# A hybrid attention and state-space layer: block 1's tokens loaded later, the output projection's weights split in phase one, four buffers for h, filler from the first slot

## The chip, the cores and the metric

The kernel runs on one core of a Trainium2 chip. The metric is the device time of one execution in microseconds (us), lower is better. Engines are named as in the profile: PE (TensorE matmul), PEld (its weight loads), DVE (VectorE), ACT (ScalarE), POOL (GpSimd), SP (SyncE, which issues nearly all DMAs, in one queue and in order).

## The reference

One layer over 2048 prompt tokens and one step of 32 sample tokens, D = 1024, eight attention heads and eight state-space (SSD) heads of 64, feed-forward width 2816:

```python
def mixer(h, k_past, v_past, ssm_h0, conv_prev, p):
    proj = h @ p['w_in']                     # q, k, v, z, xbc, dt
    ...
    attn = stick_breaking(q, q_pos, k_all, v_all, k_pos).reshape(b, l, D_ATT)
    xbc_c, conv_new = causal_dwconv(xbc, conv_prev, p['ssm_conv_w'], p['ssm_conv_b'])
    xbc_c = jax.nn.silu(xbc_c)
    ...
    y, h_fin = ssd_scan(xh, dt, a, bm, cm, ssm_h0.astype(jnp.float32))
    ...
    y = rmsnorm(y * jax.nn.silu(z), p['g_ssm_out'])
    out = jnp.concatenate([rmsnorm(attn, p['g_attn_out']), y], axis=-1) @ p['w_out']
    return out, k, v, h_fin.astype(ssm_h0.dtype), conv_new

def conv_ffn(h, conv_prev, p):
    gu = h @ p['w_up']
    gate, up = gu[..., :D_FF], gu[..., D_FF:]
    gate_c, conv_new = causal_dwconv(gate, conv_prev, p['ffn_conv_w'], p['ffn_conv_b'])
    act = jax.nn.gelu(gate_c, approximate=True) * up
    return act @ p['w_down'], conv_new

def layer(x, ...):
    m, ... = mixer(rmsnorm(x, p['g_mix_pre']), ...)
    x = x + rmsnorm(m, p['g_mix_post'])
    f, ... = conv_ffn(rmsnorm(x, p['g_ffn_pre']), ...)
    x = x + rmsnorm(f, p['g_ffn_post'])
```

Stick-breaking attention weights a key by sigmoid(z) times the product of 1 - sigmoid over the later keys, which the kernel computes with a scan along the keys.

## The kernel before

All matrices are kept transposed, features on the 128 partitions and tokens along the free axis, in blocks of 512, 512, 512 and 544 tokens (`SBS`, blocks 0 to 3; the last holds the 32 sample tokens too). A product of two float32 matrices is three matmuls: each operand is split into a high part and a low part (hi x hi, hi x lo, lo x hi), in `dense` (L173).

**Weights.** `weight` (called for one chunk of 128 output features) does one of two things. The first time, `raw` loads the float32 chunk (`wraw`, L130), and `divide` makes the high part by a cast on ACT (L153) and the low part by a subtract on POOL (L154), and SP writes both to DRAM (`wS_...`, L157) under a key. Later, `recall` (L145) loads the split pair from there. A tile of the pair is 1024 columns wide in phase one and 512 in the second phase (`unit`); a pair that was written 1024 wide can be recalled in halves under the key with "part".

**Phase one** (`phase_in`) runs per block s: six chunks of the input projection for the convolution branch (weights wbx; ACT evacuates at L403, the DVE multiplies by the row scale r at L409), the convolution on the DVE (L412, L416), silu on ACT and DVE (L388, L389), the V projection (matmuls L441, whose weight is split into wvhi by ACT, L295, and wvlo by the DVE, L296; evacuated by ACT at L448 or L450, and split for the value store by POOL at L462 and L463), the SSD scan (L487 to L596, y matmuls L569), the k and q projections, and the gate z. `prep` (L306 to L323) loads the next block's x and squares it for the norm.

**Attention and what fills it.** `heads(s)` goes through slots (head, key block, group of 128 keys): scores on the PE (z, L899), sigmoid on ACT (L747, L748), the scan prow (L750) on the DVE, a product beta (L755) on POOL or DVE, a transpose on the PE (L918) whose result ACT and DVE split (L922, L923), and the value product (L940), added up by the DVE (L955). The slot i - 2 is finished while slot i is scored (`LOOK` = 2). In between, `fill` takes units from a generator, the filler: in heads(0) the last block's gate and the sample tokens' attention, and in heads(1) to heads(3) the `Tail` of block s - 1: the output projection (`out_units`, weights "out"), its norm and the residual, the split of the normed h (L1088), the up projection with its convolution and gelu, the down projection, with the `finish` of block s - 2 spread among the up projection's units. The last block's tail runs alone at the end. A running sum `debt` gives out the units at `rate` = units / slots.

`finish` handles 256 columns at a time: for each of eight feature chunks it loads h (`xr`, L1415, SP), scales f (L1416, DVE), adds h (L1420, POOL for even chunks and DVE for odd ones) and stores the result (L1421). In heads(2) and heads(3), where it works on blocks 0 and 1, the tile for h has two buffers; the finishes after that take another pool (`late`).

**What sets the order.** The kernel is written as tiles with pools; a scheduler works out each engine's order of instructions from dependencies, the written order and its own estimates, so an edit in one place moves instructions in others. `behind` adds an order between two instructions of one queue.

Of the kernel before, what the change touches and what calls it, by code (L numbers as in the profile page):

```python
# [8 lines left out]
F32 = mybir.dt.float32  # L9
# [8 lines left out]
LOOK = 2  # L18
# [13 lines left out]
P = 128  # L32
D = 1024
KC = D // P
# [35 lines left out]
class Kernel:  # L70
# [56 lines left out]
    def raw(self, src, m):  # L127

        raw = self.wp.tile([P, self.unit, P], F32, name="wraw", bufs=self.rbufs)
        self.nc.sync.dma_start(raw[:, :m, :], src)  # L130
        return raw

    def held(self, pool, tag):
# [131 lines left out]
def phase_in(kn, ctx):  # L265
    nc, tc, a, o = kn.nc, kn.tc, kn.a, kn.o
    pool = lambda name, bufs, **kw: ctx.enter_context(tc.tile_pool(name=name, bufs=bufs, reuse_waits="tile", **kw))
# [6 lines left out]
    wp = kn.wp  # L274
# [31 lines left out]
    def prep(s):  # L306

        t0, nt = SBS[s]
        x = ep.tile([P, KC, 544], F32, name="x")
        for k in range(0, KC, 2):  # L310
            nc.sync.dma_start(x[:, k : k + 2, :nt], a["xT"][:, k : k + 2, t0 : t0 + nt])
        sq = tmp.tile([P, 544], F32, name="sq", bufs=1)
        for k in range(KC):
            if k == 0:
                nc.scalar.activation(sq[:, :nt], x[:, k, :nt], AF.Square)
            else:
                t = tmp.tile([P, 550], F32, name="t")
                nc.scalar.activation(t[:, :nt], x[:, k, :nt], AF.Square)
                nc.gpsimd.tensor_tensor(sq[:, :nt], sq[:, :nt], t[:, :nt], op=ALU.add)
        r = kn.rstd_narrow(rp, psm, "st", [sq], nt, D)  # L320
        for k in range(KC):
            nc.vector.scalar_tensor_tensor(
                x[:, k, :nt], x[:, k, :nt], kn.col(C_GMIX + k), r[:, :nt], op0=ALU.mult, op1=ALU.mult  # L323
            )
        return x
# [41 lines left out]
    for s, (t0, nt) in enumerate(SBS):  # L367
# [7 lines left out]
        raw = ep.tile([P, 6, 550], F32, name="raw")  # L375
# [16 lines left out]
        w = wfirst if s == 0 else None  # L392
        for c, then in zip(order, (*order[1:], None)):
            if w is None:
                w = kn.weight(wp, a["wbx"][c], key=("bx", c))
# [26 lines left out]
            w = ahead  # L422
# [11 lines left out]
            nc.vector.memset(u[:, 32:40], 0.0)  # L434
        for b in range(nb):
            q = min(P, nt - b * P)
            vp = [psd.tile([P, 512], F32, name="o") for _ in range(2)]
            for h in range(2):
                for k in range(KC):
                    for i, (l, rr) in enumerate(((xhi, wv[0]), (xlo, wv[0]), (xhi, wv[1]))):  # L440
                        nc.tensor.matmul(  # L441
                            vp[h][:q, :260], l[k][:, b * P : b * P + q], rr[:, k, h * 260 : h * 260 + 260],
                            start=i == 0 and k == 0, stop=i == 2 and k == KC - 1,
                        )
            v = sd.tile([P, 520], F32, name="v")
            for dst, src in ((v[:q, 0:260], vp[0][:q, :260]), (v[:q, 260:520], vp[1][:q, :260])):
                if s == 0:
                    copy = nc.scalar.activation(dst, src, AF.Copy, scale=rcol[:q, b : b + 1])  # L448
                else:
                    copy = nc.scalar.copy(dst, src)  # L450
            if b == 0:
                silu(owed, copy)
            nc.vector.tensor_tensor(
                u[:q, b * 8 : b * 8 + 8], v[:q, 512:520], kn.cv[:q, C_DTB : C_DTB + 8], op=ALU.add
            )
            tok = t0 + b * P
            nc.sync.dma_start(o["v"][tok : tok + q, :], v[:q, :512])
            if b == 4:
                nc.sync.dma_start(kn.vF[:], v[:DEC, :512])
                continue  # L460
            vs = sd.tile([P, 2, 512], F32R, name="vs", bufs=1)
            nc.gpsimd.tensor_copy(vs[:, 0, :], v[:, :512])  # L462
            nc.gpsimd.tensor_tensor(vs[:, 1, :], v[:, :512], vs[:, 0, :].bitcast(F32), op=ALU.subtract)  # L463
            for e in range(2):
                nc.sync.dma_start(
                    kn.vS[s][:, :, b, e * DH : e * DH + DH].rearrange("h p d -> p h d"),
                    vs[:, e, :].bitcast(F32).rearrange("p (h d) -> p h d", d=DH),
                )
# [228 lines left out]
class Attention:  # L697
# [172 lines left out]
    def heads(self, s, steps, every=None):  # L870

        kn, nc, kp = self.kn, self.kn.nc, self.kp
        nt = SBS[s][1]
        slots = [(h, kc, b) for h in range(NH) for kc in range(s, -1, -1) for b in range(4)]
        att, live, late = [], {}, []
        sq = None
        debt, rate = 0.0, steps / len(slots)
        cur = {}

        def scores(i):  # L880
# [80 lines left out]
        for i in range(len(slots) + LOOK):  # L961
            if i < len(slots):
                scores(i)
            if i >= LOOK:
                debt += rate
                self.fill(int(debt))
                debt -= int(debt)
                values()
                turn(i - LOOK)
                if every is not None:  # L970
                    every(i - LOOK)
# [5 lines left out]
class Tail:  # L977
# [24 lines left out]
    def out_units(self, s, cat, half):  # L1002

        kn, nc, att = self.kn, self.kn.nc, self.att
        c0, c1 = half
        if c0 == 0:
            self.Q = [[self.mp.tile([P, 4, 272], F32, name=f"n{2 * i + e}") for e in range(2)] for i in range(2)]
            self.msq = att.tmp.tile([P, 544], F32, name="sq")
            self.w = {}
        back = list(range(KC - WBUFS * UNIT // KC, KC))  # L1010
        for i, c in enumerate(range(KC) if c0 == 0 else back + list(range(back[0]))):
            m = self.m(c, half)
            w = self.w.pop(c, None)
            if w is None:
                pool = self.keep if self.keep is not None and c not in back else kn.wp
                w = kn.weight(pool, kn.a["wout"][c], key=("out", c), tag=f"w{c}" if pool is self.keep else None)
                if c0 == 0 and (c in back or pool is self.keep):
                    self.w[c] = w
            ps = self.po[0].tile([P, 512], F32, name=self.po[1])
            for k in (4, 5, 6, 7, 0, 1, 2, 3):  # L1020
                kn.dense(ps, w[k : k + 1], cat, c0, c1, k0=k, first=k == 4, last=k == 3, pin=self.pin)
                if k != 3:
                    yield
            nc.scalar.copy(m, ps[:, : c1 - c0])
            if i < KC - 1:
                att.square(self.msq[:, c0:c1], m, i == 0)
            else:
                t = att.tmp.tile([P, 272], F32, name="sqt", bufs=2)[:, : c1 - c0]
                nc.scalar.activation(t, m, AF.Square)
                self.msqs = [self.msq[:, c0:c1], t]  # L1030
            yield
# [364 lines left out]
    def finish(self, s, c0, c1, f):  # L1396
# [10 lines left out]
            yield  # L1407
        for c in range(KC):
            if not self.late:
                h = att.tmp.tile([P, 272], F32, name="xr", bufs=2)[:, :n]  # L1410
            else:
                if c % 2 == 0:
                    pair = self.late.tile([P, 548], F32, name="xr", bufs=4)
                h = pair[:, n * (c % 2) : n * (c % 2) + n]
# [239 lines left out]
```

## Time and profile before

| | before |
|---|---|
| time, median of 3 runs | 2888.32 us (2884.95 to 2894.43) |
| profiled execution, its own time | 2909.14 us |
| its span | 2907.1 us |
| its mean granted clock of the PE | 0.983 |
| phase one, about | 0 to 600 us |
| heads(0), heads(1), heads(2), heads(3), about | 600 to 710, 710 to 1240, 1240 to 1840, 1840 to 2400 us |
| last tail, about | 2400 to 2907 us |

The profile is of one execution. "Idle before, releaser" names what ended an engine's wait; windows give each engine's busy time in a stretch, with the mean clock that the PE was granted (1.00 is full speed). Two stretches of heads(1) and heads(2) do the same work on the output projection: in heads(1) its weights are split, in heads(2) recalled.

### The profile page before, as it was taken

The numbers are of one execution on the slowest core, as the hardware profiler recorded it, in microseconds if no ns is written. First come the engines' busy times: TensorE is split into PE (matmuls) and PEld (weight loads), VectorE is DVE, ScalarE is ACT, GpSimd is POOL, SyncE is SP. The second block draws the span as 40 slices with busy tenths as digits, with TensorE's granted clock in tenths as the row PEclk, the third lists the DMA queues.
The fourth block names the chain that finished last, engine by engine and source line by source line (L and its number), as shares of the span: only waits on it lengthen the run. The fifth ranks groups of instructions, "written<-read, shape, count | busy, mean of one in ns | idle before, by whom it ended". The sixth has DMA issues, their size and how long they took to land.

```text
span 2907.1 us, 46192 instructions
## 1 busy us (share of the span) xinstructions
PE 2803.7 (96%) x16771; PEld 2421.8 (83%) x16771; DVE 1644.0 (57%) x2628; ACT 1223.9 (42%) x2576; POOL 1136.7 (39%) x1073
## 2 busy tenths in 40 slices
PE   7999999988989999999999999989999999999997
PEld 6887879876878888897788888978888879899997
DVE  7685656447664554557455555775666653623333
ACT  5343434246555544455333334654444433321111
POOL 4633231226666666555222223453223224411113
PEclk9999999999999999999999999999999999999998
DMA  8878686878768877786655556666555555755556
GB/s 307 267 270 259 225 246 195 240 233 266 250 222 270 271 270 257 248 282 197 211 176 176 180 182 230 205 202 195 175 170 170 165 188 176 245 177 178 169 178 196
DMA packets 336612, 633.65 MB, mean 218 GB/s; under 512 B 73498, under 2 KB 192930, under 8 KB 327682
## 3 DMA queue, kind: packets, MB, share of 16 engines
q1 hardware_dynamic: 336386, 630.70, 66.5%
q8 instruction: 134, 2.20, 0.3%
q14 instruction: 92, 0.75, 0.1%
HBM read 474.01 MB, written 156.57 MB: 217 GB/s over the span
## 4 chain that ended last, share of the span: by engine, by line
PE 80%; DMA 7%; DVE 7%; ACT 3%; issue 2%; SPq 1%; POOL 1%; DVEq 0%; ACTq 0%; POOLq 0%
PE o L173 40%; PE u L173 12%; PE t L173 11%; PE z L899 4%; PE pa L940 4%; PE pt L918 3%; PE o L441 3%; DMA acB<-acD 1%; DVE prow L750 1%; DMA o_kT<-kf 1%; DMA eA<-acD 1%; DVE xlo L1088 1%; DMA xr<-hS 1%; DVE f L1416 1%; PE u L215 1%
## 5 line engine op out<-in xcount | busy, mean ns | idle before, releaser
L173 PE MATMUL o<-xhi,w 128*128 128x512 f32 (+2 forms) x3968 | 1047.2, 345 | 21.0 <-ACT xhi L346 7.9
L173 PEld LDWEIGHTS o<-xhi,w 128*128 128x128 f32 x3968 | 698.2, 192 | 113.8 <-ACT xhi L346 7.9
L173 PE MATMUL o<-xlo,w 128*128 128x512 f32 (+2 forms) x1984 | 682.1, 344 | 3.7 <-DVE xlo L332 2.5
L755 POOL TENSOR_TENSOR beta<-beta,prow 128x512 f32<-128x512 f32 (+3 forms) x256 | 252.0, 985 | 463.8 <-DVE prow L750 378.4
L173 PEld LDWEIGHTS o<-xlo,w 128*128 128x128 f32 x1984 | 379.7, 191 | 47.0 <-DVE xlo L332 2.9
L173 PE MATMUL u<-xhi,w 128*128 128x512 f32 x1056 | 351.3, 399 | 0.0
L173 PE MATMUL o<-ah,w 128*128 128x512 f32 x992 | 344.7, 403 | 6.2 <-DVE f L1384 6.1
L1336 POOL TENSOR_TENSOR y<-y,gb 128x512 f32<-128x512 f32 (+1 forms) x88 | 116.2, 1320 | 507.9 <-ACT gb L1335 507.8
L154 POOL TENSOR_TENSOR w<-wraw,w 128x512 fp32r<-128x512 f32 (+3 forms) x186 | 244.4, 1318 | 136.1 <-ACT w L153 116.4
L750 DVE TENSOR_TENSOR_SCAN prow<-gam,prow,z 128x513 f32<-128x513 f32 x192 | 245.3, 1278 | 79.1 <-ACT beta L748 76.3
L923 DVE TENSOR_TENSOR wt<-pt,wt 128x512 fp32r<-128x512 f32 (+2 forms) x320 | 192.0, 601 | 160.3 <-ACT wt L922 158.3
L922 ACT CAST wt<-pt 128x512 fp32r<-128x512 f32 (+2 forms) x320 | 167.8, 526 | 220.6 <-PE pt L918 219.6
L173 PEld LDWEIGHTS u<-xhi,w 128*128 128x128 f32 x1056 | 199.6, 189 | 46.9
L173 PEld LDWEIGHTS o<-ah,w 128*128 128x128 f32 x992 | 187.8, 189 | 48.9 <-DVE f L1384 8.1
L747 ACT ACTIVATE gam<-z 128x512 f32<-128x512 f32 (+2 forms) x320 | 172.4, 539 | 102.0 <-PE z L899 63.6
L173 PE MATMUL u<-xlo,w 128*128 128x512 f32 x528 | 209.9, 398 | 0.0
L173 PE MATMUL o<-al,w 128*128 128x512 f32 x496 | 197.3, 398 | 0.0
L173 PE MATMUL t<-xhi,w 128*128 128x272 f32 x960 | 189.5, 293 | 2.0 <-DMA w<-wS_up 1.4
L940 PE MATMUL pa<-wt,v 128*64 128x256 f32 (+3 forms) x1152 | 171.4, 279 | 15.3 <-DVE wt L923 6.0
L1328 DVE SCALAR_TENSOR_TENSOR y<-gb,cv,y 128x512 f32<-128x512 f32 (+1 forms) x176 | 143.5, 815 | 73.6 <-ACT y L1326 70.9
L918 PE MATMUL pt<-ident,beta 128*128 128x128 f32 x1088 | 180.6, 276 | 1.6 <-POOL beta L755 1.0
L153 ACT CAST w<-wraw 128x512 fp32r<-128x512 f32 (+3 forms) x186 | 114.4, 615 | 154.0 <-PE o L173 92.7
(288 smaller groups left out, 4895.1 us busy)
## 6 DMA issues: line engine op xcount, KB each, us to landing
w<-wS_up SPq DMA_DIRECT2D x264, 512.0 KB, 3.5
w<-wS_dn SPq DMA_DIRECT2D x144, 384.0 KB, 3.5
wS_up<-w SPq DMA_DIRECT2D x88, 512.0 KB, 3.3
w<-wS_out SPq DMA_DIRECT2D x78, 512.0 KB, 5.5
wraw<-wup SPq DMA_DIRECT2D x88, 256.0 KB, 4.0
k<-kS SPq DMA_DIRECT2D x80, 256.0 KB, 3.8
v<-vS SPq DMA_DIRECT2D x80, 256.0 KB, 3.9
w<-wS_bx SPq DMA_DIRECT2D x18, 1024.0 KB, 4.9
```

The costliest lines, as they stand in the source:

```text
L154: nc.gpsimd.tensor_tensor(lo, raw[:, :m, :], hi.bitcast(F32), op=ALU.subtract)
L173: mm = nc.tensor.matmul(ps[:, : c1 - c0], l, r, start=first and i == 0 and k == 0, stop=last and i == 2 and k == len(w) - 1, **({"skip_gro ...
L747: nc.scalar.activation(g[:, c0:512], z, AF.Sigmoid, scale=-0.125)
L750: nc.vector.tensor_tensor_scan(back(pr), back(g), z[:, 0:1].to_broadcast([P, n + 1]), self.kn.ones[:, 0:1] if prev is None else prev, op0= ...
L755: eng.tensor_tensor(b[:, :n], b[:, :n], pr[:, c0 + 1 : 513], op=ALU.mult)
L899: mm = nc.tensor.matmul(z[:, :n], q[:, P * b : P * b + P], k[:, :n], start=e == 0, stop=e == 1 and kc < s)
L918: mm = nc.tensor.transpose(t[:, P * j : P * j + P], w[:, P * j : P * j + P], kn.ident[:])
L922: nc.scalar.copy(hi, t)
L923: nc.vector.tensor_tensor(lo, t, hi.bitcast(F32), op=ALU.subtract)
L940: nc.tensor.matmul(av[:m, 2 * P * p + c0 : 2 * P * p + 2 * P], v[:, j, :m], wt[:, rest, j, c0:], start=kc == s and p + j + rest == 0, stop ...
L1328: nc.vector.scalar_tensor_tensor(y[:, :W], gb[:, i : i + W], kn.col(wc + i), y[:, :W], op0=ALU.mult, op1=ALU.add)
L1336: nc.gpsimd.tensor_tensor(y[:, :W], y[:, :W], t, op=ALU.mult)
```

## The change

Four edits. (1) `raw` remembers its load, and the four loads of block 1's x are put behind the load that was the last at that point, the sixth chunk of wbx. (2) In phase one, blocks 1 to 3, ahead of the V projection, eight chunks of wout are loaded, split 1024 wide and written under a new key, and the output projection recalls them in halves. The sixteen splits of 512 columns under the old key are gone. SP's recalls of these weights go from 78 to 94, each of 512 KB, and the writes from sixteen of 512 KB to eight of 1 MB. (3) `xr` has four buffers instead of two in the finishes of blocks 0 and 1. (4) The filler is called in every slot, the first two included, and the rate is worked out for the slots and these two.

```diff
     def raw(self, src, m):
 
         raw = self.wp.tile([P, self.unit, P], F32, name="wraw", bufs=self.rbufs)
-        self.nc.sync.dma_start(raw[:, :m, :], src)
+        self.load = self.nc.sync.dma_start(raw[:, :m, :], src)
         return raw
...
         for k in range(0, KC, 2):
-            nc.sync.dma_start(x[:, k : k + 2, :nt], a["xT"][:, k : k + 2, t0 : t0 + nt])
+            load = nc.sync.dma_start(x[:, k : k + 2, :nt], a["xT"][:, k : k + 2, t0 : t0 + nt])
+            if s == 1:
+                kn.behind(load, kn.load)
...
         for b in range(nb):
             q = min(P, nt - b * P)
+            if 0 < s and b < 3 and 3 * s - 3 + b < KC:
+                kn.weight(wp, a["wout"][3 * s - 3 + b], key=("outw", 3 * s - 3 + b))
...
-        debt, rate = 0.0, steps / len(slots)
+        debt, rate = 0.0, steps / (len(slots) + LOOK)
...
             if i < len(slots):
                 scores(i)
+            debt += rate
+            self.fill(int(debt))
+            debt -= int(debt)
             if i >= LOOK:
-                debt += rate
-                self.fill(int(debt))
-                debt -= int(debt)
                 values()
...
-                w = kn.weight(pool, kn.a["wout"][c], key=("out", c), tag=f"w{c}" if pool is self.keep else None)
+                w = kn.weight(pool, kn.a["wout"][c], key=("outw", c, "part"), tag=f"w{c}" if pool is self.keep else None)
...
             if not self.late:
-                h = att.tmp.tile([P, 272], F32, name="xr", bufs=2)[:, :n]
+                h = att.tmp.tile([P, 272], F32, name="xr", bufs=4)[:, :n]
```

The lines of the kernel after the change stand a few lower: L412, L416 and L389 are L414, L418 and L391 there, and from L441 on four lower (L755 is L759, L848 is L852, L860 is L864, L1420 is L1424).

The first place is the DVE in the first block, from the third L296 on (wvlo, the low part of the V weight; raw is a chunk of the input projection, xc and bc the convolution's outputs). Before, the fourth L296:

```order
L416 SCALAR_TENSOR_TENSOR xc<-raw,cv,xc 128x512 x2
L296 TENSOR_TENSOR wvlo<-wvraw,wvhi 128x1040
L409 TENSOR_TENSOR raw<-raw,r_231 128x512
L389 TENSOR_TENSOR xc<-xc,t 128x512
L537 TENSOR_TENSOR cbm<-y,triu 128x256
L412 TENSOR_SCALAR xc<-raw,cv 128x512
L427 COPY hist<-raw 128x18
L416 SCALAR_TENSOR_TENSOR xc<-raw,cv,xc 128x512 x3
L453 TENSOR_TENSOR u<-v,cv 128x8
```

and in the changed kernel, with the rows around the same L296:

```order
L411 TENSOR_TENSOR raw<-raw,r_231 128x512
L418 SCALAR_TENSOR_TENSOR xc<-raw,cv,xc 128x512
L414 TENSOR_SCALAR xc<-raw,cv 128x512
L429 COPY hist<-raw 128x18
L391 TENSOR_TENSOR xc<-xc,t 128x512
L541 TENSOR_TENSOR cbm<-y,triu 128x256
L418 SCALAR_TENSOR_TENSOR xc<-raw,cv,xc 128x512 x3
L296 TENSOR_TENSOR wvlo<-wvraw,wvhi 128x1040
L391 TENSOR_TENSOR xc<-xc,t 128x512
L418 SCALAR_TENSOR_TENSOR xc<-raw,cv,xc 128x512
L381 COPY raw<-hist 128x6x3
L457 TENSOR_TENSOR u<-v,cv 128x8
```

The fourth L296 moves behind the multiply of the last input chunk and nearly all of its convolution.

The second place is POOL in heads(1) (w is a weight's low part, xlo the low part of the attention's output, sq a sum of squares, n the residual). Before:

```order
L755 TENSOR_TENSOR beta<-beta,prow 128x512 x2
L154 TENSOR_TENSOR w<-wraw,w 128x512 x3
L860 TENSOR_TENSOR sq<-sq,sqt 128x256
L848 TENSOR_TENSOR xlo_7256<-att,xhi_7248 128x256
L848 TENSOR_TENSOR xlo_7257<-att,xhi_7249 128x256
L154 TENSOR_TENSOR w<-wraw,w 128x512
L848 TENSOR_TENSOR xlo_7258<-att,xhi_7250 128x256
L848 TENSOR_TENSOR xlo_7259<-att,xhi_7251 128x256
L154 TENSOR_TENSOR w<-wraw,w 128x512
L860 TENSOR_TENSOR sq<-sq,sqt 128x256
L154 TENSOR_TENSOR w<-wraw,w 128x512 x3
L860 TENSOR_TENSOR sq<-sq,sqt 128x256
```

and now:

```order
L759 TENSOR_TENSOR beta<-beta,prow 128x512 x2
L864 TENSOR_TENSOR sq<-sq,sqt 128x256
L852 TENSOR_TENSOR xlo_7312<-att,xhi_7304 128x256
L852 TENSOR_TENSOR xlo_7313<-att,xhi_7305 128x256
L852 TENSOR_TENSOR xlo_7314<-att,xhi_7306 128x256
L852 TENSOR_TENSOR xlo_7315<-att,xhi_7307 128x256
L864 TENSOR_TENSOR sq<-sq,sqt 128x256 x5
L238 TENSOR_TENSOR rn_v<-rn_v,mhalf 128x2
```

The eight subtracts of wout that stood here have gone; their place in the changed kernel is ahead of the V projection's rows (L466, before L462) of blocks 1 to 3, three, three and two of them, 1024 wide.

The third place is the DVE in heads(2), in the finish of block 0 (f is the down projection's result, xr the loaded h). Before:

```order
L1420 TENSOR_TENSOR f_14630<-f_14630,xr 128x256
L750 SCALAR_TENSOR_TENSOR prow<-gam_5839,prow,z 128x513
L1349 TENSOR_TENSOR y<-u,y 128x512
L1420 TENSOR_TENSOR f_14632<-f_14632,xr 128x256
L1315 TENSOR_TENSOR gb<-o,r 128x512
L1420 TENSOR_TENSOR f_14634<-f_14634,xr 128x256
L232 SCALAR_TENSOR_TENSOR rn_v<-u,rcol_13726 128x2
```

and now:

```order
L1424 TENSOR_TENSOR f_14590<-f_14590,xr 128x256
L1424 TENSOR_TENSOR f_14592<-f_14592,xr 128x256
L1424 TENSOR_TENSOR f_14594<-f_14594,xr 128x256
L1353 TENSOR_TENSOR y<-u,y 128x512
L1424 TENSOR_TENSOR f_14596<-f_14596,xr 128x256
L1319 TENSOR_TENSOR gb<-o,r 128x512
L232 SCALAR_TENSOR_TENSOR rn_v<-u,rcol_13661 128x2
```

The four adds stand closer together, all four ahead of the row scale's L232 where three stood.

On the PE, at the end of phase one, the first y group (L569) of the last block has 43 dense matmuls directly ahead of it where 25 stood, and between the last y group and the first attention scores there are 18 where 81 stood.

## The prediction

> **What bounds the kernel now.** I read the page first (busy times, slices, chain), then windows for each stage, then the waits of the PE, and last the timelines around its longest waits.
>
> ```profile
> PE 2803.7 (96%) x16771; PEld 2421.8 (83%) x16771; DVE 1644.0 (57%) x2628; ACT 1223.9 (42%) x2576; POOL 1136.7 (39%) x1073
> ...
> PE 80%; DMA 7%; DVE 7%; ACT 3%; issue 2%; SPq 1%; POOL 1%; DVEq 0%; ACTq 0%; POOLq 0%
> core 0: us, PE busy (x) PEld busy (x) DVE busy (x) ACT busy (x) POOL busy (x), PEclk, DMA share, GB/s
> 94.00:545.00 451.00, 446.15 (x2698) 376.22 (x2697) 278.98 (x529) 170.02 (x290) 153.58 (x116) 1.00 0.78 246
> 545.00:580.00 35.00, 29.52 (x262) 25.92 (x262) 26.40 (x81) 11.83 (x24) 7.85 (x6) 1.00 0.88 274
> 712.00:770.00 58.00, 50.04 (x351) 45.58 (x349) 39.57 (x61) 34.76 (x81) 36.14 (x41) 0.88 0.63 215
> 1240.00:1290.00 50.00, 48.21 (x395) 46.87 (x394) 25.46 (x42) 27.03 (x69) 23.89 (x29) 1.00 0.78 266
> 1352.00:1392.00 40.00, 35.63 (x171) 28.96 (x170) 27.90 (x45) 15.28 (x34) 16.41 (x16) 0.91 0.60 191
> ```
>
> The PE is the bound. In the profiled execution it is idle for 2907.1 - 2803.7 = 103.4 us of the span, and the number of matmuls does not change, so the change can win only out of those 103 us and out of time at a lower granted clock. A window's loss is its idle time plus (1 - clock) times its length: 712 to 770, where the second block's attention begins and block 0's output projection runs as filler, loses 7.96 + 0.12 x 58 = 14.9 us. The matching stretch of the third block, 1240 to 1290, which only recalls split weights, loses 1.8. Most of phase one (94 to 545) loses 4.85 in 451. So the four edits touch short, known places, and what each is worth is read there.
>
> **Start: x of block 1 behind the last input-projection weight.**
>
> ```profile
> 21.31 2.47 SPq L311 DMA_DIRECT2D x<-xT  x4
> 39.14 0.51 PE L173 MATMUL o<-xhi,w 128*128 128x512 f32 x1 [1.48 <-ACT w L153]
> 43.04 1.22 PE L173 MATMUL o<-xhi,w 128*128 128x512 f32 x2 [3.17 <-POOL w L154]
> 41.76:48.59 6.83, 5.55 (x13) 4.40 (x14) 6.47 (x7) 4.86 (x6) 3.27 (x2) 0.50 0.68 233
> ...
> 32.95 1.90 DVE L409 TENSOR_TENSOR raw<-raw,r 128x512 f32<-128x512 f32 x3 [2.66 <-ACT r L260]
> 47.04 2.69 DVE L389 TENSOR_TENSOR bc<-bc,t 128x512 f32<-128x512 f32 x1
> 51.47 0.68 DVE L389 TENSOR_TENSOR xc<-xc,t 128x512 f32<-128x512 f32 x1
> 61.16 1.24 DVE L296 TENSOR_TENSOR wvlo<-wvraw,wvhi 128x1040 fp32r<-128x1040 f32 x1
> 68.80 0.16 DVE L453 TENSOR_TENSOR u<-v,cv 128x8 f32<-128x8 f32 x1
> 62.33 0.28 PE L441 MATMUL o<-wvlo,xhi 128*128 128x260 f32 x1
> 71.42 0.39 PE L441 MATMUL o<-wvhi,xhi 128*128 128x260 f32 x1 [1.53 <-ACT v L448]
> ```
>
> The four x loads now go out behind the last two weight loads, so weight chunk five comes some 3 us or more earlier, and its cast and subtract are ready before the PE needs them. That removes 1.48 + 3.17 us of idle and half of the 6.83 us at clock 0.50: 8.1 us, up to the V matmuls. There the DVE is late next. From 32.95, when the row scale r is ready, to 69 its instructions adjoin, so it has no room to follow a faster PE. Five of them are stretched by some 2.0 us each while POOL runs a 1024-wide subtract (L389: 2.69 against 0.68). The first matmul on the low part of the fourth V weight starts at 62.33, and L296 that makes this part ends at 62.40: no slack. The PE would now arrive at 62.4 - 8.1 = 54.3. But the new order puts that L296 behind all of the conv work except two products (0.68 each), one tap (0.74) and some copies (0.35). At the old pace it would start at 69.0 - 1.24 - 1.36 - 0.74 - 0.35 = 65.3 and end at 66.5. One POOL subtract less beside it: 64.5. With no stretching at all, 56.5. At 64.5 the PE waits 10 us, passes that point 2.1 us later than before, pays about 3.4 us for half a clock after the wait, and saves the 1.53 behind L448: -2.1 - 3.4 + 1.5 = -4. The ends are 62.4 - 66.5 - 3.4 + 1.5 = -6 and, with half of that clock, 62.4 - 56.5 - 1.7 + 1.5 = +5.7; their middle is 0. As POOL's subtracts also move, I take **-2 us**, between that middle and the pace that the rows show: the gain does not survive V.
>
> **Output projection's weights.** Sixteen casts and sixteen subtracts of 512 columns (some in the first block's attention) become eight of 1024 in phase one, and sixteen more recalls of 512 KB.
>
> ```profile
> 712.00:770.00 58.00, 11.42 (x9) 0.88 0.63 215
> 747.40 3.74 POOL L154 TENSOR_TENSOR w<-wraw,w 128x512 fp32r<-128x512 f32 x3
> 745.05 7.32 DVE L755 TENSOR_TENSOR beta<-beta,prow 128x512 f32<-128x512 f32 x1
> 753.02 1.01 PE L940 MATMUL pa<-wt,v 128*128 128x256 f32 x4 [4.21 <-DVE att L955]
> 751.70:758.50 6.80, 5.48 (x24) 5.29 (x25) 5.03 (x6) 2.18 (x4) 2.49 (x4) 0.50 0.34 116
> w<-wS_out SPq DMA_DIRECT2D x78, 512.0 KB, 5.5
> ...
> 26.79 2.41 POOL L154 TENSOR_TENSOR w<-wraw,w 128x1024 fp32r<-128x1024 f32 x1
> 210.00:220.00 10.00, 10.00 (x86) 10.00 (x86) 1.43 (x3) 5.41 (x11) 8.92 (x9) 1.00 0.52 137
> ```
>
> The first row is POOL at line 154 alone: nine subtracts, 11.42 us, in the stretch that loses 14.9. The next four show how it becomes a loss: POOL runs subtracts back to back, a DVE product beside them takes 7.32 us, the accumulation behind it (L955) is late, the PE waits 4.21 and then runs 6.8 us at half clock. That one chain is 4.21 + 3.4 = 7.6 us. Without the subtracts it goes; at most, the stretch falls to the 1.8 of its twin: 13.1. What is late next are the attention's own prow waits, which hold the rest of the idle time there. Ends 0 (the DVE stays the bound) and 13; I take **10**, between the proven chain and the twin. The twin also had its recalls (5.5 us each) in time with the DMA at 0.78.
>
> In phase one, eight subtracts of 2.41 us stand on POOL ahead of the V matmuls of blocks 1 to 3, three, three and two. The cover: after the conv work the DVE is busy for only 1.43 of 10 us (210 to 220), so some 3 x 2.0 = 6 us of stretching fits into the 8.6 free. SP's new writes stand ahead of the recalls for k and are ready some 20 us before the PE needs these. Without that cover the cost is 17 + 10 us (third rival). I take **-1**, ends 0 and -6.
>
> **End of phase one.**
>
> ```profile
> PE o L173 <- ACT kf L364: 2.8, 2, 1.7
> PE y L569 <- DVE acB L541: 2.2, 1, 2.2
> ```
>
> From 545 to 580 the PE loses 5.5 us, most of it in these waits around the last block's scan. The new order has 43 dense matmuls ahead of its first y group where 25 stood, and 18 instead of 81 between the last y group and the first attention scores. That covers the scan better and the attention's start less. Ends -2 and +5.5; I take **+3**.
>
> **Four buffers for h.**
>
> ```profile
>   POOL f L1420: 9.3, 4
>   DVE f L1420: 4.0, 3
> ...
> DMA to landing us min/median/max: 2.2/2.7/4.8
> 1381.70 0.73 PE L940 MATMUL pa<-wt,v 128*128 128x256 f32 x4 [2.55 <-ACT wt L922]
> 1383.70 1.22 PE L250 MATMUL u<-ident,rn_v 128*128 128x128 f32 x4 [1.26 <-POOL rn_v L238]
> 1953.18 0.42 DVE L1420 TENSOR_TENSOR f<-f,xr 128x256 f32<-128x256 f32 x1 [2.69 <-DMA xr<-hS]
> 1954.96 0.71 PE L250 MATMUL u<-ident,rn_v 128*128 128x128 f32 x4 [3.17 <-POOL rn_v L238]
> ```
>
> With two buffers each load waits for an add, and each add for its load (2.7 us). In the third block's attention the DVE and POOL stand so for 4.0 and 9.3 us; behind the adds wait attention's multiply and the row scale, and the PE loses 2.55 + 1.26 and 0.09 x 40 = 3.6 of clock. In the fourth block it is 3.17. Together 10.6 us. With four buffers the first four loads are in flight at once and the last four still go one behind another's add; one wait of about 2.7 in three stays for each engine. Ends 0 and 10.6; I take **6**.
>
> A rule to weigh: the Trainium skill, "TensorE: Matmul & The Clock Gate", section "What's actually happening", has the clock halved only after about 3.4 us idle. By that rule the pair 2.55 + 1.26 need cost no clock, and this term would be some 3 us smaller; the 0.91 in the row decides against it.
>
> **Filler from the first slot.** The same units are spread over two more slots, so nothing is added or removed; the first two slots of each attention get filler that the last two lose. No row shows its price; the nearest are the waits at the attention's starts, a few us each. 0, ends -4 and +4.
>
> **Sum.** -2 + 10 - 1 + 3 + 6 + 0 = 16 us. The profiled execution took 2909.1, 20.8 us above the median of the runs (2888.3): 2893 on its own scale, and as the terms are mostly fixed waits, 2888.3 - 16 = **2872** for the median.
>
> **Rivals.** (1) *The DVE at the start, at full price*: -6 instead of -2, 2876. For it: DVE rows that adjoin for 36 us. Against: the order of POOL's subtracts moves too. (2) *The attention chain is the bound in 712 to 770 whatever POOL does*: 3 instead of 10, 2879. For: the PE also waits there on prow. Against: the twin's 1.8. (3) *Slower: the eight subtracts shut the DVE out in phase one.* Each stretches a DVE instruction by 2.0 to 2.4 us; if all eight reach the PE, 17 us and, with a wait in each of three blocks, three times 3.4 of clock: 27, against 17 from the rest: 2898. It decides where less than 6 us of the DVE are free between the conv and the V results; the row at 210 has 8.6. The Trainium skill, "SBUF — State Buffer", section "SBUF: two separate sides", speaks for it: GpSimd and a two-input DVE instruction take a shared port by an exclusive lock for a whole instruction. The 7.32 us agree, and are longer than one subtract; by the rule eight subtracts could cost the DVE an estimated 8 x 2.41 = 19 us. (4) *The buffers do nothing*, as the loads are issued behind SP's other work: 0 instead of 6, 2878. (5) *More*: no stretching at the start (+5.7) and all 10.6 at the finish, 16 + 7.7 + 4.6 = 28 us, 2860.
>
> **How the numbers follow.** Forecast 0.40; (5) 0.15; (1) 0.13; (2) 0.12; (4) 0.07; two of (1), (2), (4) together, about 2884, 0.05; (3) 0.08. A measurement of this kernel tells about 0.3%, 8.7 us, from no change: below 2879.6 lie the forecast, (5) and, by their spread, two thirds of the single rivals: 0.76; within 0.16; slower 0.08. The range 2855 to 2884 leaves out (3) and the tails.
>
> **What would show it.** Right: no wait behind L153 or L154 before 45 us, but one of about 10 us at the V matmuls on L296; 712 to 770 losing under 6 us; DVE and POOL waiting half as long on xr. Wrong: V entered at 50 us without a wait; new PE waits on the DVE between 180 and 545; a 4 us wait still there near 750.

## The result, and the profile after

| | before | after |
|---|---|---|
| time, median of 20 runs each | 2894.89 us (2884.95 to 2904.13) | 2901.14 us (2895.73 to 2907.68) |
| ratio of the times | | 1.0019, 95% interval 1.001 to 1.0028 |
| profiled execution, its own time | 2909.14 us | 2902.53 us |
| its span, its mean granted clock | 2907.1 us, 0.983 | 2900.7 us, 0.984 |

The change makes the kernel some 5 us slower (0.19% of 2895 is 5.5), where 16 us faster was forecast. The two profiles say the opposite: the one of after is 6.4 us shorter. Twenty runs show why: the profiled execution of before lies 14 us above the median of its own kernel and outside the range of the twenty. So a wait that was read in that execution need not be the kernel's.

The head of the changed kernel's page:

```profile
span 2900.7 us, 46190 instructions
PE 2795.4 (96%) x16771; PEld 2415.3 (83%) x16771; DVE 1658.1 (57%) x2628; ACT 1218.4 (42%) x2568; POOL 1134.3 (39%) x1065
```

The PE is still the bound, at the same 96%. The windows that the prediction used (length, then PE, PEld, DVE, ACT and POOL busy, clock, DMA share, GB/s), with one more, 600 to 715, the first block's attention, in the changed kernel:

```profile
94.00:545.00 451.00, 440.82 (x2625) 371.23 (x2624) 294.05 (x526) 173.90 (x294) 167.32 (x123) 0.99 0.82 269
545.00:580.00 35.00, 35.00 (x294) 31.96 (x294) 20.65 (x58) 10.21 (x21) 10.00 (x8) 1.00 0.94 299
600.00:715.00 115.00, 97.57 (x715) 76.27 (x712) 73.72 (x113) 65.99 (x171) 43.16 (x58) 0.94 0.83 262
712.00:770.00 58.00, 52.10 (x369) 46.44 (x368) 28.33 (x57) 30.64 (x72) 26.36 (x32) 0.88 0.54 172
1352.00:1392.00 40.00, 38.57 (x202) 32.16 (x201) 29.34 (x49) 14.74 (x32) 19.88 (x19) 1.00 0.69 220
```

The same windows of a second profile of the kernel before, taken for this study (below, before_again; span 2895.0 us):

```profile
94.00:545.00 451.00, 446.26 (x2693) 376.56 (x2692) 279.12 (x526) 169.87 (x289) 153.01 (x115) 1.00 0.78 245
545.00:580.00 35.00, 29.29 (x257) 25.86 (x257) 26.35 (x82) 11.85 (x24) 7.55 (x6) 1.00 0.88 274
600.00:715.00 115.00, 100.90 (x737) 78.61 (x735) 75.95 (x128) 74.35 (x187) 56.53 (x69) 0.96 0.87 282
712.00:770.00 58.00, 54.71 (x407) 51.07 (x407) 33.83 (x63) 36.41 (x86) 37.85 (x43) 0.91 0.72 244
1352.00:1392.00 40.00, 35.21 (x156) 28.38 (x156) 24.87 (x45) 11.31 (x26) 16.69 (x17) 0.91 0.65 193
```

Read the PE's busy time (second number) against the window's length. Four of the five agree between before's two profiles, 94 to 545 and 545 to 580 within 0.3 us, 1352 to 1392 within 0.5, and 600 to 715 (99.47 in the first) within 1.5. But 712 to 770, on which the largest term of the prediction rests, has 54.71 busy here and 50.04 in the first profile. Against the second profile, the change gains 5.7 us at the end of phase one, and 3.4 at 1352 to 1392 with its clock beside it (0.91 to 1.00); it loses 5.4 us idle and some clock in 94 to 545, 3.3 and some clock in the first attention, and 2.6 and some clock at 712 to 770.

### The profile page after: what moved, and what is told of

It reads as the page before. It is cut to its first block, busy times and chain, and to the rows that moved or that the text cites. A ratio compares the mean times of both kernels' runs of the same rounds, so it can differ in the third digit from the quotient of the medians.

```text
span 2900.7 us, 46190 instructions
## 1 busy us (share of the span) xinstructions
PE 2795.4 (96%) x16771; PEld 2415.3 (83%) x16771; DVE 1658.1 (57%) x2628; ACT 1218.4 (42%) x2568; POOL 1134.3 (39%) x1065
## 4 chain that ended last, share of the span: by engine, by line
PE 75%; DMA 9%; DVE 9%; issue 2%; ACT 2%; POOL 1%; SPq 1%; DVEq 0%; POOLq 0%; ACTq 0%
PE o L173 38%; PE u L173 12%; PE t L173 10%; PE z L903 4%; PE pa L944 4%; PE pt L922 3%; DVE xc L418 1%; PE o L445 1%; DVE prow L754 1%; DMA w<-wS_outw 1%; DMA vS<-vs 1%; DVE xlo L1092 1%; DVE f L1420 1%; DMA xr<-hS 1%; PE u L215 1%
## 5 line engine op out<-in xcount | busy, mean ns | idle before, releaser
L759 POOL TENSOR_TENSOR beta<-beta,prow 128x512 f32<-128x512 f32 (+3 forms) x256 | 255.3, 998 | 510.6 <-DVE prow L754 426.7
L154 POOL TENSOR_TENSOR w<-wraw,w 128x512 fp32r<-128x512 f32 (+3 forms) x178 | 243.3, 1369 | 152.4 <-ACT w L153 131.4
L922 PE MATMUL pt<-ident,beta 128*128 128x128 f32 x1088 | 182.9, 277 | 5.0 <-DVE wt L927 5.0
L153 ACT CAST w<-wraw 128x512 fp32r<-128x512 f32 (+3 forms) x178 | 113.0, 635 | 155.4 <-PE o L173 98.8
```

Of the source, the lines that this page charges most:

```text
L154: nc.gpsimd.tensor_tensor(lo, raw[:, :m, :], hi.bitcast(F32), op=ALU.subtract)
L759: eng.tensor_tensor(b[:, :n], b[:, :n], pr[:, c0 + 1 : 513], op=ALU.mult)
L922: mm = nc.tensor.transpose(t[:, P * j : P * j + P], w[:, P * j : P * j + P], kn.ident[:])
```

## The experiments

Eighteen runs, each timed against the kernel before on the same chip. For a ratio, 0.001 is 2.9 us.

### Each edit alone

The four kernels have the lines of one edit of the diff each, the others as before.

> Only the first edit: block 1's x behind the last input-projection weight. If the DVE's chain of the first block is the next limit, the two waits behind L153 and L154 near 40 us go and a wait of 8 to 10 us on the low and high parts of the V weight appears near 55 to 62 us: no gain, 0 to 4 us slower. If the gain of the start survives V, 4 to 8 us faster.

> Only the second edit: the eight splits of wout in phase one. By the prediction 9 us faster: 712 to 770 loses 10 us less and phase one 1 more. If the 4.2 us wait and its half clock near 750 us belonged to the one profiled execution and not to the kernel, and the V evacuations of blocks 1 to 3 now wait for ACT (about 2 us each, and half clock after two of them), it is 0 to 8 us slower.

> Only the third edit: four buffers for h. By the prediction 6 us faster, with POOL and DVE waiting half as long on xr near 1370 us; if the adds were hidden in most executions anyway, within 2 us of before.

> Only the fourth edit: filler from the first slot. By the prediction 0. If it brings the sample tokens' scores forward to where their cached keys have not landed (in the changed kernel the PE waits 11.6 us for sk in 600 to 712 us, before it 3.1), 4 to 9 us slower.

| one edit alone | ratio | 95% interval | us against before |
|---|---|---|---|
| block 1's x later | 1.0003 | 0.9992 to 1.0014 | +1 |
| output projection's weights | 0.9995 | 0.9986 to 1.0005 | -1 |
| four buffers for h | 0.9976 | 0.9962 to 0.9989 | -7 |
| filler from the first slot | 1.0016 | 1.0005 to 1.0026 | +5 |

Two terms hold: x (forecast -2 us of gain, measured -1; the PE waits 7.8 us for the V weight, near the 8 to 10 expected) and h (forecast 6, measured 7). Two fail: the weights are worth nothing, and the filler costs.

The gain at the end of phase one, a term of its own in the prediction, comes with the weights. The window 545 to 580 in the two profiles of the weights alone (the second was taken later, below):

```profile
545.00:580.00 35.00, 33.51 (x277) 30.29 (x276) 18.48 (x53) 10.82 (x23) 9.32 (x7) 1.00 0.93 292
```

```profile
545.00:580.00 35.00, 33.34 (x275) 30.32 (x273) 17.13 (x47) 10.40 (x22) 10.75 (x8) 1.00 0.92 276
```

The PE is busy for 4 us more than in the two profiles of before (29.5 and 29.3); with x alone or h alone the window still loses some 5 us. So the nothing that the weights are worth is a sum of gains and losses, which are looked for below.

### Each edit left out

> Edits 1 to 3 without the filler's. If the four edits only add up, 0.9 - 1.4 - 7 = 7.5 us faster than before (ratio 0.9974). If the loss comes of edits working against each other and not of the filler, it stays near 2900, at 0 to 4 us slower than before. The waits for sk (11.6 us in the changed kernel, 600 to 712 us) fall to about 3 in the first case.

> Edits 1, 3 and 4 without the output projection's. If edits add up, 0.9 - 7 + 4.6 = 1.5 us faster than before. If the early splits of wout turn against the rest (the V evacuations in blocks 1 to 3 waiting, the sample's keys late), 8 to 10 us faster than the changed kernel, which is 3 to 5 us faster than before.

> Edits 2 to 4 without block 1's x. If edits add up, -1.4 - 7 + 4.6 = 3.8 us faster than before. If putting x later costs more together with the early splits (SP's queue in phase one), 8 us or more faster than the changed kernel.

> Edits 1, 2 and 4 with two buffers for h. If the four buffers are worth the same 7 us here as alone, 12 us slower than before (ratio 1.0043). If their gain is lost in the changed kernel, about the same as the changed kernel, 5 us slower than before.

| three edits, without | ratio | 95% interval | us against before |
|---|---|---|---|
| the filler | 0.9978 | 0.9965 to 0.9992 | -6 |
| the output projection's weights | 1.0010 | 0.9996 to 1.0025 | +3 |
| x | 1.0040 | 1.0026 to 1.0054 | +12 |
| four buffers for h | 1.0026 | 1.0013 to 1.0040 | +8 |

Leaving out the filler turns the loss into a gain; leaving out anything else does not. The edits do not add up, though: the four alone sum to some -3 us against before, together they are +5. The filler costs 5 us alone and 12 on top of the other three. Without x or without the weights, neither branch of the expectation came true; x, worth nothing alone, seems to be worth 6 us beside the other three (1.0040 against 1.0019, with intervals that overlap a little). Without h the interval (4 to 12 us slower) holds both branches.

### The filler and the sample's keys

In the first block's attention a step of the sample tokens' attention runs after every third slot; its keys (sk) are loaded by SP into two buffers (from ck, the cached keys, and kF, the new ones). The load stands at L799 and the score matmul that reads the keys at L802; before, at L795 and L798. The waits of the PE at that matmul in 600 to 715 us (total, times, longest), first of the changed kernel, then of the three edits without the filler:

```profile
PE z L802 <- DMA sk<-ck: 6.9, 3, 3.9
PE z L802 <- DMA sk<-kF: 4.7, 1, 4.7
```

```profile
PE z L802 <- DMA sk<-kF: 2.2, 1, 2.2
PE z L802 <- DMA sk<-ck: 0.4, 1, 0.4
```

And what SP, whose queue is in order, waited for at its key loads, in the changed kernel and in the first profile of before:

```profile
SPq L799 <- PE z L802: 9.2, 4, 3.5
```

```profile
SPq L795 <- PE z L798: 5.3, 5, 2.7
```

SP stands at a key load until the matmul that uses the buffer has run; the load is then late for the next matmul, and what stands behind it in SP's queue is late too. With the filler from the first slot the PE stands 11.6 us for keys, without it 2.6. The first block's attention, from its first score matmul to the first of the second block's, takes 104.8 us in the changed kernel and 98.5 in the three edits without the filler (100.4 and 98.1 in the two profiles of before).

With the filler alone it shows less. The PE's waits at the sample's score matmul there:

```profile
PE z L798 <- DMA sv<-cvv: 2.5, 1, 2.5
PE z L798 <- DMA sk<-kF: 1.5, 1, 1.5
PE z L798 <- DMA k<-kS: 1.4, 1, 1.4
```

The first and the last are waits for keys too: the PE's weight load directly ahead of each ends a wait for `sk<-ck` (2.8 and 2.2 us) at the same moment. That makes 5.4 us, against 3.1 before, and the first attention takes 98.8 us, no more than before. So the measured 5 us lie in the expected 4 to 9, but this profile, of the fastest of its twelve runs, shows no price in the first attention; where the filler alone loses its 5 us is open.

Three kernels test the price beside the other edits. Two switch the filler by block:

```diff
-        debt, rate = 0.0, steps / (len(slots) + LOOK)
+        debt, rate = 0.0, steps / (len(slots) + (LOOK if s else 0))
...
-            debt += rate
-            self.fill(int(debt))
-            debt -= int(debt)
+            if s or i >= LOOK:
+                debt += rate
+                self.fill(int(debt))
+                debt -= int(debt)
```

(and with `not s` and the rate the other way round), and one changes the keys' buffers in the changed kernel:

```diff
-                    k = kp.tile([P, 512], F32, name="sk", bufs=2)
+                    k = kp.tile([P, 512], F32, name="sk", bufs=4)
```

> The changed kernel, but the first block's attention gives its filler as before (from the third slot). If the filler's price is the sample tokens' keys that come late in the first block's attention, it is as fast as the kernel without the filler edit: about 6 us faster than before (0.998), with waits for sk of about 3 us in 600 to 715 us. If the price lies in the later blocks' attention, it stays near the changed kernel, 5 us slower than before.

> The changed kernel, but only the first block's attention gives filler from the first slot; the later three as before. If the price is the sample's keys, it stays 5 us slower than before, with 7 to 12 us of waits for sk; if it lies in the later blocks, 6 us faster than before.

> The changed kernel with four buffers instead of two for the sample's cached keys (sk). If the PE waits for sk because a key load may only start when the matmul before last has given its buffer back, the waits for sk fall from 11.6 to under 4 us and the kernel gains 5 to 10 us on the changed one: from even with before to 5 us faster. If the loads are late for another reason (SP's queue, the DMA's load), the waits stay and the time too.

| | ratio | 95% interval | us against before |
|---|---|---|---|
| changed kernel, filler not in the first attention | 0.9999 | 0.9990 to 1.0007 | 0 |
| changed kernel, filler only there | 1.0018 | 1.0006 to 1.0029 | +5 |
| changed kernel, four key buffers | 0.9976 | 0.9967 to 0.9986 | -7 |

The first attention carries much of the price: with the edit only there the time is that of the changed kernel (5 us slower, as expected), and with it everywhere else 5 us come back. The PE's waits for keys go along: 9.3 us with the filler only there, 2.3 with it everywhere else. But that second kernel is not at 0.998, where the three edits without the filler are: in the later blocks the edit seems to cost some 6 us too, though the two intervals overlap a little. With four buffers the keys' waits of the PE come down to this row, the waits on the `ck` loads are gone, the first attention takes 98.9 us instead of 104.8, and the kernel gains 12 us (5 to 10 were expected):

```profile
PE z L802 <- DMA sk<-kF: 4.1, 1, 4.1
```

The keys were short of buffers before the change too, so the same edit was tried without the change, alone and with four buffers for h, and with and without the filler:

> Only the four buffers for h, and four instead of two for the sample's keys; nothing else changed. If the keys' buffers matter only once the filler has brought the scores forward, as fast as with four buffers for h alone, 7 us faster than before (0.9976); if the keys are late in the kernel before too (PE and PEld wait 4.7 us for them there), 9 to 12 us faster.

> Edits 1 to 3 and four buffers for the sample's keys, filler as before. If the filler from the first slot is worth something once the keys are in time, this is slower than the changed kernel with four key buffers (0.9976); if it is worth nothing, the same as that or up to 4 us faster.

> The kernel before with four buffers for the sample's keys and nothing else. If the two buffer edits add up, the 24 us of both less the 7 of h alone: 17 us faster than before (0.994). If the 24 came of an order of instructions that only the two together give, within 6 us of before.

> Four buffers for h, four for the sample's keys, and filler from the first slot. If the filler's price is only that the keys were late, the same as without the filler (0.992, 24 us faster than before) within 4 us. If filler from the first slot costs by itself, 8 to 15 us slower than that.

| four key buffers and | ratio | 95% interval | us against before |
|---|---|---|---|
| nothing else | 0.9957 | 0.9943 to 0.9972 | -12 |
| four buffers for h | **0.9918** | 0.9898 to 0.9938 | **-24** |
| four buffers for h and the filler | 0.9960 | 0.9944 to 0.9976 | -12 |
| edits 1 to 3 | 0.9989 | 0.9976 to 1.0003 | -3 |

Two changed numbers, four buffers for h and four for the keys, beat both kernels: 2873.95 us (median of 6) against 2895.26. Four key buffers alone gain 12 us, where 17 or under 6 had been expected. With these alone the first attention takes 91.8 us, and SP's waits for the key matmuls at L795 (5.3 and 5.7 us in the two profiles of before) are gone, while the PE's own waits for keys hardly change (2.5 us against 3.1 and 2.9). So the gain lies in what stands behind the key loads in SP's queue more than in the keys. One rival stays: the scheduler gives all five queues another order from about 610 us on when the tile has four buffers, and no run has the buffers without the new order.

The windows of the kernel with both, in which the same work stands some 10 us earlier than before by 700 us:

```profile
600.00:715.00 115.00, 103.05 (x785) 82.59 (x783) 85.48 (x145) 80.42 (x203) 61.57 (x75) 0.96 0.93 305
715.00:770.00 55.00, 54.71 (x448) 52.66 (x446) 34.93 (x56) 38.89 (x98) 41.39 (x45) 1.00 0.76 257
```

and with the filler besides:

```profile
600.00:715.00 115.00, 97.60 (x742) 78.82 (x742) 82.74 (x138) 77.25 (x195) 57.47 (x70) 0.94 0.90 291
715.00:770.00 55.00, 53.62 (x417) 50.47 (x418) 30.77 (x54) 35.04 (x85) 39.48 (x45) 0.96 0.72 235
...
PE z L798 <- DMA sk<-kF: 5.4, 1, 5.4
```

The filler from the first slot loses 5.5 us more in the first attention here too, one wait of 5.4 on the first keys among it (2.6 without the filler), and the time is 12 us longer. So here the filler costs by itself, as the second branch of the expectation (8 to 15 us) had it, and the late buffers are not its whole price. But with edits 1 to 3 and four key buffers the filler does not cost at all: 0.9976 with it, 0.9989 without it, with intervals that overlap. What it is worth depends on the order that the scheduler makes of the rest. That edits 1 and 2 cost some 20 us on top of the two buffer edits (0.9989 against 0.9918), though each is worth nothing alone, was not foreseen either, and its cause is open.

### Where the output projection's 10 us were

The term rested on one chain in the first profile, with a DVE product of 7.32 us. The order of POOL's instructions at this place is the same in the second profile of before and in the kernel with four buffers for h alone. In the second profile of before, the DVE product and POOL's subtract at this place:

```profile
745.20 0.99 DVE L755 TENSOR_TENSOR beta<-beta,prow 128x512 f32<-128x512 f32 x1
...
745.60 1.73 POOL L154 TENSOR_TENSOR w<-wraw,w 128x512 fp32r<-128x512 f32 x1
```

and in the kernel with four buffers for h alone:

```profile
747.70 7.30 DVE L755 TENSOR_TENSOR beta<-beta,prow 128x512 f32<-128x512 f32 x1
```

It is one race. In all three the product begins while POOL works at L848. In the second profile of before it gets in ahead of the next subtract, which then takes 1.73 us instead of 1.3; in the two others it stays out over that subtract and all that POOL has behind it without a break, and ends when POOL pauses. Which of the two comes about differs from execution to execution of one program. The Trainium skill, "SBUF — State Buffer", section "Who interferes with whom", says that a DVE instruction with two SBUF inputs and a GpSimd instruction that reads SBUF contend for a shared port and that the order of issue decides who is blocked; 0.99 and 1.73 on the one hand and 7.30 on the other agree with that.

> The kernel before, unchanged, profiled a second time. If the first profile of it (2909.1 us, 14 us above the median of twenty runs) showed losses that belong to that one execution, the idle time and half clock of 600 to 900 us (46.8 us there) come out 10 us or more lower, most of it in the clock. If the losses are the kernel's own, they come out within 3 us. The time is that of before, ratio 1.000 within 0.001.

> The second edit alone, profiled and timed a second time. Its first profile loses 33.8 us in 600 to 900, 13 less than the first of before, but its time was only 1.4 us lower. If the edit removes a wait of its own, 600 to 900 again loses about 10 less than the second profile of before, and the time is 3 to 6 us lower in this second measurement; if the two first profiles were a slow and a fast execution, the second ones differ by under 5 and the time is within 2 us of before.

| | ratio | 95% interval |
|---|---|---|
| before, unchanged | 0.9990 | 0.9975 to 1.0006 |
| output projection's weights alone, again | 0.9997 | 0.9983 to 1.0010 |

In the second profile of before, 600 to 900 us loses 9 us less than in the first (10 or more had been expected), most of it idle time and not clock. The second profile of the edit alone loses 2 us less there than that, and its time is that of before: the 13 us that lay between the two first profiles in this stretch were nearly all of the executions and not of the edit, as the second branch of the expectation had it.

The stretch 712 to 770 in the two profiles of the edit alone:

```profile
712.00:770.00 58.00, 54.76 (x413) 50.84 (x414) 30.82 (x61) 30.96 (x78) 27.57 (x35) 0.94 0.63 206
```

```profile
712.00:770.00 58.00, 54.02 (x407) 48.87 (x406) 28.73 (x62) 29.13 (x70) 26.36 (x34) 0.94 0.60 194
```

By the prediction's own measure (idle and the share of clock) the stretch loses 14.9 us in the first profile of before, 8.5 in the second (3.29 + 0.09 x 58), and 6.7 and 7.5 without the subtracts. The edit is worth 1 to 2 us there in an execution that wins the race, 7 to 8 in one that loses it. Phase one, in the same two profiles of the edit alone, is where the rest goes:

```profile
94.00:545.00 451.00, 439.62 (x2619) 369.76 (x2618) 290.33 (x521) 175.35 (x294) 165.36 (x121) 0.99 0.81 267
```

```profile
94.00:545.00 451.00, 441.39 (x2595) 371.20 (x2594) 287.47 (x520) 175.04 (x294) 165.32 (x121) 0.98 0.81 266
```

446.2 in both profiles of before, 440.5 here: 5.7 us idle, and a clock of 0.98 to 0.99 instead of 1.00, by the prediction's measure 4.5 to 9 us more. Of this 4 us come back at 545 to 580. The mechanism, in the three edits without the filler, block 1, around the V matmuls: DVE, POOL, ACT, PE in this order.

```profile
206.40 2.77 DVE L391 TENSOR_TENSOR xc<-xc,t 128x512 f32<-128x512 f32 x1
209.09 3.67 DVE L418 SCALAR_TENSOR_TENSOR xc<-raw,cv,xc 128x512 f32<-128x512 f32 x2
...
205.91 5.51 POOL L154 TENSOR_TENSOR w<-wraw,w 128x1024 fp32r<-128x1024 f32 x2 [4.05 <-ACT w L153]
...
212.86 0.63 ACT L390 ACTIVATE t<-xc 128x512 f32<-128x512 f32 x1 [4.64 <-DVE xc L418]
...
213.80 0.39 PE L445 MATMUL o<-wvhi,xhi 128*128 128x260 f32 x1 [1.81 <-ACT v L454]
```

Beside two new subtracts the DVE's product for the silu (L391) takes 2.77 us where 0.68 is normal, the two convolution taps behind it (L418) 3.67 where two take 1.5; ACT waits 4.64 us for these at the next silu, the V evacuation (L454) stands behind this silu in ACT's queue, and the PE waits for the evacuation. In the changed kernel these waits add up to this:

```profile
PE o L445 <- ACT v L454: 5.8, 3, 2.1
```

To test it, the splits were put behind the evacuation and the value split of the same tokens (edits 1 to 3 otherwise):

```diff
+            if 0 < s and b < 3 and 3 * s - 3 + b < KC:
+                kn.weight(wp, a["wout"][3 * s - 3 + b], key=("outw", 3 * s - 3 + b))
+                kn.behind(kn.cast, copy)
+                kn.behind(kn.sub, vsub)
```

> Edits 1 to 3 with the eight casts and subtracts of wout put behind the evacuation and the value split of the same 128 tokens, where the DVE has little to do, instead of ahead of the V matmuls. If POOL's subtracts stretch the convolution's DVE work and hold up ACT's V evacuations, the PE's waits for L454 in blocks 1 to 3 (5.4 us, and half clock after some) go: 4 to 8 us faster than edits 1 to 3 (which are 6.4 us faster than before). If the stretching was hidden all the same, no difference from these.

It is slower: 1.0053 (1.0041 to 1.0065), 15 us against before. The PE's waits for the V evacuation are gone from its list of waits for 100 to 600 us, as expected. What stands in their place is headed by

```profile
PE o L173 <- DMA w<-wS_wk: 4.3, 2, 3.0
PE o L173 <- ACT kf L366: 3.2, 1, 3.2
PE st L587 <- POOL xw L565: 2.7, 1, 2.7
```

The recalls of the k weights now stand behind the later split's write in SP's queue, and POOL's work for k and the scan behind its subtracts. The mechanism at V is shown: neither profile of before has a PE wait for the V evacuation in 100 to 600 us, and with the splits moved it is gone again. That there is room behind V is not shown: both places are taken.

## Why the prediction was wrong, point by point

- **Start: right.** L296 was forecast to end at 64.5, with a wait of 10 us at V. In the changed kernel:

```profile
62.81 1.23 DVE L296 TENSOR_TENSOR wvlo<-wvraw,wvhi 128x1040 fp32r<-128x1040 f32 x1
...
58.95 0.52 PE L445 MATMUL o<-wvhi,xhi 128*128 128x260 f32 x1 [3.92 <-ACT wvhi L295]
64.09 0.59 PE L445 MATMUL o<-wvlo,xhi 128*128 128x260 f32 x1 [3.98 <-DVE wvlo L296]
```

  The first row is the DVE's, the others the PE's. L296 ends at 64.04, and the PE waits 7.9 us in two pieces (the high part is late too, behind a silu of ACT that waits for the DVE). The waits of 1.48 and 3.17 us behind L153 and L154 are gone, and the edit alone is worth nothing. As was said, the gain does not survive V.
- **Output projection in 712 to 770: the step that failed most.** "That one chain is 4.21 + 3.4 = 7.6 us. Without the subtracts it goes" took what one execution had lost for what the kernel loses, although the prediction itself had that execution at 20.8 us above the median. The twin's 1.8 us was no bound either: without the subtracts the stretch still loses 6.7 and 7.5 us, so the term was 1 to 2 us in an execution that wins the race, 7 to 8 in one that loses it, and not 10; how often it is lost is not known. Rival 2 had the place right and kept 3 us.
- **Output projection in phase one: too small.** The cover was looked for in the wrong queue. The DVE was indeed free after 210 us, but ACT's evacuations stand behind silus that wait for the stretched DVE work ahead of that. Forecast -1, end -6; the windows show 5.7 us of idle time and 4.5 to 9 of clock. Rival 3 named the mechanism; 10 to 15 us of its 27 came about.
- **End of phase one: right, at its upper end.** 3 forecast, 5.5 in the window with all edits. Its rows agree in both profiles of before. The weights alone bring 4 of it.
- **Four buffers for h: right.** 6 forecast, 7 measured alone; the 2.55 behind L922 is gone and 1352 to 1392 runs at full clock in the changed kernel (0.96 with the four buffers alone). POOL waits a third as long on the loads and the DVE about half as long, as was said. Their waits in 1340 to 1420 us, which holds the sixteen loads of a `finish`, in the first profile of before and in the changed kernel:

```profile
  POOL f L1420: 15.4, 6
  DVE f L1420: 12.5, 6
```

```profile
  DVE f L1424: 7.0, 3
  POOL f L1424: 5.5, 3
```

  The second profile of before has 16.3 and 13.4, the four buffers alone 4.7 and 7.0. The 9.3 and 4.0 that the prediction showed are of 1352 to 1392, where only nine of the sixteen loads stand.
- **Filler from the first slot: the sign was wrong.** It was taken at 0 with ends of 4 us because no row showed its price. It costs 5 us alone, 12 on top of the other three. Rows that pointed there were to be had: PE and SP waiting for the sample's keys, with two buffers, in just the attention that the edit changes. Beside the other three edits these waits grow from 2.6 to 11.6 us, and four key buffers bring back 12 us of time; alone they grow from 3.1 to 5.4 only, and the rest of the price is open.
- **Sum.** By the single edits x loses 1 us, the weights gain 1, h gains 7 and the filler loses 5: a gain of about 3, and together they lose 5. The eight us between belong to no single edit. Most of them come with the filler (12 us on top of the other three, 5 alone). The longer waits for keys beside the other edits are a part of that; why it costs more there is otherwise open. As an estimate from these numbers, of the 21 us between the forecast and the time the stretch at 712 to 770 makes 8 to 9, phase one some 5, and the filler 5 to 12.

## What to carry to other kernels

Before a term is taken from a chain of waits in one profile, compare that execution's time with the kernel's runs, and look for the chain in a second profile: here the first lay 14 us above the runs, and the second did not have the chain of the largest term. Compare waits in windows that hold the whole of the work: in one that ends too soon they come out too short. Work that is moved to an engine with idle time still has to be followed into the queues of the others: POOL's subtract stretches the DVE, the DVE holds up a silu, and behind the silu stands the evacuation that the PE needs. And where an in-order queue stands at a load for want of a buffer, one more pair of buffers can be worth more than moving work about: two numbers gave 24 us here, with the new order that came of them.

## What the runs showed of the hardware

- The same DVE product of two operands, at the same place of the same order, took 0.99 us in one profile and 7.30 and 7.32 in two others. It was shut out over six POOL instructions that followed each other without a break (four subtracts of 1.3 us and two sums of 0.7), not over one.
- The PE's granted clock fell to about 0.91 over 1352 to 1392 us in both profiles of before, where no single wait was longer than 3.7 us, and stayed at 1.00 in the changed kernel, where the longest single wait was 1.3 us.
- The span of one unchanged kernel's profiled execution was 2907.1 and 2895.0 us; twenty runs of it spread over 19 us.
